# A first loop of three feature units over 1024 tokens, the sample's tile by column quarters, and the gate input copied out of its bank first

## The chip, the cores and the metric

The kernel runs on one core of a Trainium2 chip. The metric is device time in microseconds (us), the median of three runs. TensorE (PE) does the matrix products, VectorE (DVE), ScalarE (ACT) and GpSimd (POOL) the rest; SyncE (SP) issues most of the transfers. Matrix products add up in eight banks of PSUM, each of 128 partitions by 512 words of 32 bits.

## The reference, cut to what matters

One layer of a streaming encoder is run on 1024 prompt tokens and 32 sample tokens with the same weights. The part before the mixers is a modulated input and one wide projection whose columns go to three mixers (mLSTM, forgetting attention called fox here, gated MLP called gMLP):

```python
mod = silu(c) @ w_ada + b_ada                 # 6 x 1024 values for each of the two sequences
sh1, sc1, g1, sh2, sc2, g2 = split(mod, 6)
h = x * (1 + sc1) + sh1                       # x: 1024 + 32 tokens, 1024 features
mq, mk, mv, mo, mi, mf, fq, fk, fv, ff, gu, gv = split(h @ w_in, ...)
# mq, mk, mv, mo, gu, gv: 256 columns each; fq, fk, fv: 512; mi, mf: 4; ff: 8
vn = layer_norm(gv); hg = gu * (tril(ws) @ vn + bs)     # gMLP, in chunks of 128 tokens
```

The three mixers' outputs go through one output projection and a layer norm, and then through a SwiGLU feed-forward with a second layer norm. mk is scaled by 1/8 before the mLSTM uses it.

## The kernel before, in words

The tokens are one row of 1056 columns: 1024 of the prompt and the last 32 of the sample. Products are made with three passes: an operand is split into a rounded high part (fp32r) and a rest, and high x high, high x rest and rest x high are added (`gemm`, L122 to L130, and L295 to L297). `weights` (L103) loads raw weights into a ring of three buffers (`RAW`), casts the high part on ACT (L115) and subtracts for the rest on DVE or POOL (L116), each part into a ring of three (`WB`).

`fm_first` (L254) is the first loop. For each of eight k (128 features each) it makes one unit of the modulation (`ada`, L182: two halves of 512 KB of `w_ada`, sixteen TensorE instructions at L190, a copy at L193, two transposes at L196, a reduction and additions), modulates x (`h1`, L222: the load of x, L228, the casts L233, the rests L234, the sample's 32 columns in plain f32 as `hs`, L235), and adds two units of 128 output features (mq) into six banks: 512 columns, then 272 and 272, where the last 272 hold the sample. `ada(k + 1)` stands ahead of `h1(k)` in the program. The sums are copied out at L276 and L278 and stored at L280.

After the loop come units of two kinds. A `fm_unit` has 128 output features for all tokens in four parts (256, 256, 272, 272); mk is two of these, `k0` and `k1p` in `ORDER` (the p says that POOL subtracts). A `tm_unit` (L282) has token tiles of 128 as rows and 256 or 264 output columns; tiles 0 to 7 are prompt, tile 8 is the sample, made by `sample_tile` (L300) in plain f32: k modulo 4 goes to one of four strips of 32 partitions of a bank, and ACT and DVE then add the four strips (L308 to L311). Units of this kind are v of fox (twice, from `w_in_v`), v and o of the mLSTM, and the gate's two halves, G0 and G2 (`evac_gv`, L357) and G1 and G3 (`evac_gmlp`, L719).

`ORDER` is the sequence in which units (q, k, v, o, G), fox heads (f), mLSTM steps (m), further modulation units (a) and small stages (g, S, s) are emitted; f and m have higher priority, and the others fill between them. A list scheduler with a modelled timeline makes each engine's order from that. The order on an engine, SP's queue of transfers included, is then fixed.

Of the kernel before, what the change touches and what calls it, by code (L numbers as in the profile page):

```python
# [15 lines left out]
P = 128  # L16
D = 1024
KT = 8
S = 1024
T = 1056  # L20
NS = 32
# [15 lines left out]
XB, AB = (3, 6)  # L37
# [1 line left out]
MLB = (1, 2, 3, 4, 5)  # L39
RESE = "pp"  # L40
TAFF = ("aaaaaaaa", "aaaaaaav")
ORDER = "q0 f0 g q1 a f1 a g S q2 f2 k0 k1p s a q3 f3 a v q4 f4 a q5 f5 o a m0 G0 q6 f6 a m1 G1p G2p q7 m2 f7 a m3 G3"
FP = (0, 0)
RAW = 3
WB = 3
# [22 lines left out]
class Kernel:  # L68
# [184 lines left out]

    def fm_first(self, src):  # L254

        self.phase = "fm"
# [3 lines left out]
        w = None  # L260
        self.ada(0, self.p0, "araw", AB, self.pt, "t")
        for k in range(KT):
            if k < KT - 1:
                self.ada(k + 1, self.p0, "araw", AB, self.pt, "t")
            self.h1(k)
            self.phase = "fm"
            if w is None:
                w = self.weights(src, KT, 256)
            for (m, o, n), ps in zip(parts, banks):
                h, l = self.h1parts(o, n)  # L270
                self.gemm(ps[:, :n], w[k:k + 1], slice(m * P, (m + 1) * P), lambda _: h(k), lambda _: l(k),
                          start=k == 0, stop=k == KT - 1)
        out = [self.t(self.p0, [P, T], F32, "h", 2) for _ in range(2)]
        for (m, o, n), ps in zip(parts, banks):
            if m:
                self.nc.vector.tensor_copy(out[m][:, o:o + n], ps[:, :n])  # L276
            else:
                self.nc.scalar.copy(out[m][:, o:o + n], ps[:, :n])  # L278
        for m in range(2):
# [20 lines left out]
    def sample_tile(self, w, ncol, evac):  # L300

        nc = self.nc
        ps = self.t(self.pg, [P, 512], F32, "g")
        for k in range(KT):
            q = slice(k % 4 * 32, k % 4 * 32 + 32)
            nc.tensor.matmul(ps[q, :ncol], self.hs[:, k, :], w[k], start=k < 4, stop=k >= 4)
# [4 lines left out]
        nc.vector.tensor_tensor(r[:32], ps[:32, :ncol], r[:32], ALU.add)  # L311
# [45 lines left out]
    def evac_gv(self, tt, ps, n):  # L357
        nc = self.nc
        st = self.t(self.sm, [P, 6], F32, "bst", 2)
        mv = self.t(self.sm, [P, 2], F32, "bmv", 2)  # L360
        nc.vector.bn_stats(st[:n], ps[:n, :256])
        nc.vector.bn_aggr(mv[:n], st[:n])
        r = self.t(self.sm, [P, 1], F32, "brs", 2)
        self.rstd(r[:n], mv[:n, 1:2], self.eps5[:n], self.sm, "brt")
        v = self.t(self.sm, [P, 256], F32, "traw", 2)
        nc.vector.tensor_scalar(v[:n], ps[:n, :256], mv[:n, 0:1], r[:n], ALU.subtract, ALU.mult)  # L366
# [40 lines left out]
    def head_unit(self, h):  # L407

        nc = self.nc
        w = self.weights(self.d["w_in_f"][2 + h], KT, P)  # L410
# [12 lines left out]
        nc.scalar.copy(k1[lo], ps[hi])  # L423
        nc.scalar.activation(q2[lo], ps[lo], AF.Copy, scale=0.125)
        for o in (0, 256):
            kr = self.t(self.sq, [P, 272], F32, "qkr", 2)
            nc.scalar.copy(kr[hi, :256], ps[hi, o:o + 256])
            self.store(self.d["o_kT"][h, :, o:o + 256], kr[hi, :256])
        self.store(self.dqh[h, hi, :512], f(k1[hi]))
        self.lastq = self.store(self.dql[h, hi, :512], f(k2[lo]))  # L430
        if h < QD:
            evac = self.evac_qk(h)
            self.phase = "fm"
            for o, n in self.ranges((1,)):
                ps = self.t(self.pg, [P, 512], F32, "g")
                self.gemm(ps[:, :n], w, slice(0, P), *self.h1parts(o, n))
                evac(o, n, ps[:, :n])
# [280 lines left out]

    def evac_gmlp(self, tt, ps, n, bank=None):  # L719
        nc = self.nc  # L720
        if tt == 8 or tt % 2 == 0:
            self.gu = self.t(self.sm, [P, 2, 256], F32R, "vhl", 2).bitcast(F32)
            self.gbank = bank or ps
        u, z = self.gu, self.gbank
        nt = 1 if tt == 8 else 2
        nc.scalar.copy(u[:n, tt % 2], ps[:n, :256])
        if tt % 2 == 0 and tt < 8:
            return
        t0 = tt - nt + 1
# [3 lines left out]
        for g in range(4):  # L733
            q = slice(64 * g, 64 * g + 64)
            nc.tensor.matmul(z[:, :, q], self.wsp[:n, g, :n], vn[:n, :nt, q], start=True, stop=True)
# [11 lines left out]
        o = t0 * P - GO[c]  # L747
# [638 lines left out]
    def run(self):  # L1386
# [45 lines left out]
        self.fm_first(w2[0])  # L1432
        s0.close()
        after = ExitStack()
        after.enter_context(tc.issue_after(self.lastx.ins))
# [27 lines left out]
        def emit(x):  # L1463
            eng = nc.gpsimd if x[-1] == "p" else nc.vector
            x = x.rstrip("p")
            i = int(x[1:] or 0)
            if x[0] == "g":
                next(gates, None)
                return ()
            if x[0] == "f":  # L1470
                return self.fox(i, ((0, 1, 2, 3),))
            if x[0] == "m":
                return self.mlstm(i)
            if x[0] == "q":
                self.head_unit(i)
            elif x[0] == "k":
                self.fm_unit(w3[i], self.evac_mqk(2 + i, 0.125), eng=eng)
            elif x[0] == "S":
                self.sample_decay()
            elif x[0] == "G":  # L1480
                self.tm_unit(w2[3 + i % 2], 256, (self.evac_gv, self.evac_gmlp)[i % 2],
                             range(4 * (i // 2), 4 + i // 2 * 5), eng=eng)
            elif x[0] == "s":
                self.mlstm_states()
            elif x[0] == "a":
                more(1)
            else:
                self.tm_unit(w2["-vo".index(x)], 256, self.evac_raw((None, self.dmv, self.dmo)["-vo".index(x)]), eng=eng)
            return ()

        for x in ORDER.split():
# [13 lines left out]
        with tc.issue_after(self.lastq.ins):  # L1505
            self.wo_mix(0, self.KORDER[0][:6])
        for h in range(QD, PRE):
            self.fm_unit(w3[2 + h], self.evac_qk(h), (1,))
        self.wo_mix(0, self.KORDER[0][6:])
        self.z[0] = self.t(self.pz, [P, KT, GN[0]], F32, "z0", 1)  # L1510
        self.pn = self.pool("pn")
# [7 lines left out]
            weave(self.wo_range(st, *MM[0][1], (2, 6, 7, 3, 4, 5, 0, 1), kept, pw), self.ln1(0, st, *MM[0][0]))  # L1519
        weave(self.ln1(0, st, *MM[0][1]))  # L1520
        for h in range(PRE, 8):
            self.fm_unit(w3[2 + h], self.evac_qk(h, True), (1,))
        self.ln1_res(0)
        s1.close()
        s4 = ExitStack()
# [116 lines left out]
def _layout(inputs):  # L1642
# [35 lines left out]
    a["w_in"] = units(np.concatenate([mq, mv, mo, gv, gu], axis=1), 256)  # L1678
    a["w_in_f"] = units(np.concatenate([mk, qk], axis=1), 128)
# [56 lines left out]
```

## Time and profile before

| | us |
|---|---|
| median of 3 runs (lowest, highest) | 1361.67 (1360.25, 1362.21) |
| the profiled execution, its time | 1363.44 |
| its span | 1360.6 |
| TensorE busy in the span | 1328.2 (98%) |
| DVE, ACT, POOL busy | 994.9, 659.6, 233.2 |
| mean granted TensorE clock | 0.995 |

The span is the time from the first to the last instruction of the profiled execution. A TensorE row has a duration that holds the way through the array, so rows overlap, and the pace is read from the starts. One plain f32 product counts as two TensorE instructions. In the name `tm_g`, tm is the stage that allocated the tile and g its tag: g, t, s and o are PSUM banks.

### The profile page before, as it was taken

What the parts mean: (1) busy time and instruction counts of PE and PEld (TensorE: products, weight loads), DVE (VectorE), ACT (ScalarE), POOL (GpSimd) and SP (SyncE); (2) the same over time, 40 slices, a digit from 0 to 9 for tenths busy, and PEclk for the clock granted to TensorE, in tenths of its full rate; (3) what the DMA queues carried; (4) which work ended last, traced back from release to release, by engine and by line L of the source; (5) the groups of instructions that cost most, each with busy time, mean ns of one, the idle gap of its engine ahead of it and who ended that gap; (6) DMA issues with size and microseconds to landing.
All of it is one profiled execution on the core that took longest, in us unless ns stands there. A gap on an engine that the chain in (4) does not pass through costs nothing.

```text
span 1360.6 us, 25153 instructions
## 1 busy us (share of the span) xinstructions
PE 1328.2 (98%) x9434; PEld 1207.9 (89%) x9434; DVE 994.9 (73%) x2103; ACT 659.6 (48%) x1304; POOL 233.2 (17%) x263
## 2 busy tenths in 40 slices
PE   7999999998999999999999999999999999999996
PEld 4798988998989778888888888999999999999995
DVE  5545654678768668686776766778998988889777
ACT  3324454455436554545445355436663554545355
POOL 0202100053226300000000000273710000000341
PEclk9999999999989999999999999999999999999999
DMA  9775565546464866354433423674596758563321
GB/s 360 250 252 162 163 197 146 177 127 200 149 206 135 208 190 181 105 156 126 135 107 114 117 90 100 204 179 128 161 259 166 205 153 220 142 176 126 98 80 66
DMA packets 120376, 221.70 MB, mean 163 GB/s; under 512 B 18740, under 2 KB 64464, under 8 KB 120256
## 3 DMA queue, kind: packets, MB, share of 16 engines
q1 hardware_dynamic: 113024, 207.55, 48.6%
q0 software_dynamic: 6032, 11.94, 5.2%
q8 instruction: 74, 1.21, 0.4%
q10 hardware_dynamic: 1200, 0.62, 0.2%
q14 instruction: 46, 0.38, 0.1%
HBM read 188.13 MB, written 51.85 MB: 176 GB/s over the span
## 4 chain that ended last, share of the span: by engine, by line
PE 87%; DVE 5%; DMA 4%; ACT 2%; issue 1%; SPq 1%; DVEq 0%; ACTq 0%
PE up_g L130 6%; PE up_g L128 6%; PE up_g L129 6%; PE dn_g L128 4%; PE dn_g L130 4%; PE dn_g L129 4%; PE tm_g L295 3%; PE tm_g L297 3%; PE tm_g L296 3%; PE sup_u L130 3%; PE sup_u L128 3%; PE sup_u L129 3%; PE wo_g L129 2%; PE fox_t L830 2%; PE wo_g L130 2%; PE wo_g L128 2%
## 5 line engine op out<-in xcount | busy, mean ns | idle before, releaser
L128 PE MATMUL up_g<-tm_ah,up_whi 128*128 128x512 f32 (+1 forms) x384 | 140.3, 365 | 1.2 <-DVE up_sil L1186 0.8
L129 PE MATMUL up_g<-tm_al,up_whi 128*128 128x512 f32 (+1 forms) x384 | 140.8, 367 | 0.0
L130 PE MATMUL up_g<-tm_ah,up_wlo 128*128 128x512 f32 (+1 forms) x384 | 139.8, 364 | 0.5 <-DVE up_wlo L116 0.5
L1255 ACT CAST sup_whi<-sup_raw 128x1024 fp32r<-128x1024 f32 x54 | 56.0, 1048 | 90.8 <-PE dn_u L129 47.4
L115 ACT CAST up_whi<-up_raw 128x1024 fp32r<-128x1024 f32 x50 | 52.5, 1049 | 68.3 <-PE up_g L129 26.1
L128 PEld LDWEIGHTS up_g<-tm_ah,up_whi 128*128 128x128 f32 x384 | 72.2, 188 | 13.7 <-DVE up_sil L1186 1.0
L130 PEld LDWEIGHTS up_g<-tm_ah,up_wlo 128*128 128x128 f32 x384 | 72.3, 188 | 11.7 <-DVE up_wlo L116 1.2
L129 PEld LDWEIGHTS up_g<-tm_al,up_whi 128*128 128x128 f32 x384 | 72.2, 188 | 10.6
L116 DVE TENSOR_TENSOR up_wlo<-up_raw,up_whi 128x1024 fp32r<-128x1024 f32 x50 | 66.6, 1333 | 13.3 <-ACT up_whi L115 12.2
L1086 DVE SCALAR_TENSOR_TENSOR wo_z<-dn_g,start_mod,wo_z 128x512 f32<-128x512 f32 (+4 forms) x120 | 60.3, 520 | 22.0 <-PE dn_g L130 21.3
L1256 DVE TENSOR_TENSOR sup_wlo<-sup_raw,sup_whi 128x1024 fp32r<-128x1024 f32 x54 | 68.2, 1266 | 10.8 <-ACT sup_whi L1255 10.8
L130 PE MATMUL dn_g<-up_acth,dn_wlo 128*128 128x512 f32 (+2 forms) x200 | 73.7, 369 | 0.0
L129 PE MATMUL dn_g<-up_actl,dn_whi 128*128 128x512 f32 (+2 forms) x200 | 73.4, 368 | 0.0
L128 PE MATMUL dn_g<-up_acth,dn_whi 128*128 128x512 f32 (+2 forms) x200 | 73.4, 368 | 0.0
L803 ACT ACTIVATE fox_p<-fox_s,fox_fmx 128x384 f32<-128x384 f32 (+2 forms) x96 | 55.1, 578 | 37.5 <-DVE fox_fmx L801 29.4
L115 ACT CAST dn_whi<-dn_raw 128x1024 fp32r<-128x1024 f32 (+1 forms) x44 | 42.7, 971 | 55.6 <-PE up_g L129 14.4
L798 DVE TENSOR_REDUCE fox_fmx<-fox_s 128x1 f32<-128x384 f32 (+2 forms) x96 | 52.6, 552 | 20.3 <-PE fox_s L795 19.3
L835 ACT CAST fox_pth<-fox_t 128x512 fp32r<-128x512 f32 (+1 forms) x80 | 41.6, 543 | 51.1 <-PE fox_t L830 49.0
L116 DVE TENSOR_TENSOR dn_wlo<-dn_raw,dn_whi 128x1024 fp32r<-128x1024 f32 (+1 forms) x44 | 49.5, 1126 | 12.9 <-ACT dn_whi L115 12.2
L836 DVE TENSOR_TENSOR fox_ptl<-fox_t,fox_pth 128x512 fp32r<-128x512 f32 (+1 forms) x80 | 49.8, 631 | 10.0 <-ACT fox_pth L835 9.7
L295 PE MATMUL tm_g<-tm_whi,start_h1h 128*128 128x256 f32 (+1 forms) x192 | 55.1, 287 | 1.9 <-DVE tm_traw L366 1.7
L296 PE MATMUL tm_g<-tm_wlo,start_h1h 128*128 128x256 f32 (+1 forms) x192 | 55.2, 288 | 0.0
(666 smaller groups left out, 4796.5 us busy)
## 6 DMA issues: line engine op xcount, KB each, us to landing
up_raw<-w_gu SPq DMA_DIRECT2D x50, 512.0 KB
dn_raw<-w_dn SPq DMA_DIRECT2D x28, 512.0 KB
ada_late<-w_ada SPq DMA_DIRECT2D x24, 512.0 KB
sup_raw<-w_gu SPq DMA_DIRECT2D x20, 512.0 KB
start_dp<-w_gu SPq DMA_DIRECT2D x19, 512.0 KB
start_dp<-w_gu POOLq DMA_DIRECT2D x19, 512.0 KB, 7.8
wo_raw<-w_o SPq DMA_DIRECT2D x18, 512.0 KB
sup_raw<-start_dp SPq DMA_DIRECT2D x18, 512.0 KB
```

Source lines behind the costliest of these rows:

```text
L115: nc.scalar.copy(hi[:, :w], raw[:, :w])
L116: (eng or nc.vector).tensor_tensor(lo[:, :w], raw[:, :w], f(hi[:, :w]), ALU.subtract)
L128: nc.tensor.matmul(ps, hi, xh(k), start=start and k == 0, stop=False)
L129: nc.tensor.matmul(ps, hi, xl(k), start=False, stop=False)
L130: self.lastmm = nc.tensor.matmul(ps, lo, xh(k), start=False, stop=stop and k == n - 1)
L295: nc.tensor.matmul(ps[:, :ncol], xh, hi, start=k == 0, stop=False)
L296: nc.tensor.matmul(ps[:, :ncol], xh, lo, start=False, stop=False)
L798: nc.vector.tensor_reduce(mxs[:, x:x + 1], s[:, :w], AX.X, ALU.max, negate=True)
L803: nc.scalar.activation(pr[:, lo:hi], banks[x][:, :hi - lo], AF.Exp, bias=mxs[:, 0:1], accum_out=sums[:, x:x + 1])
L1086: self.lastz = self.nc.vector.scalar_tensor_tensor(z[:, m, x:y], ps[:, x - a:y - a], g[i], z[:, m, x:y], ALU.mult, ALU.add)
L1255: nc.scalar.copy(h, x)
L1256: tt(l, x, f(h), ALU.subtract)
```

## The change

The first loop takes three units (mq and the first half of mk) over the 1024 prompt tokens alone, as six parts of 512 columns. Its weights come in four chunks of two k each, 768 columns wide, and `h1(k)` and the chunk's load stand ahead of `ada(k + 1)`. The sample's 32 tokens are made from `hs` and the raw weights: after each fourth k, one matmul for each of the four k writes a strip of 32 partitions, and ACT copies the strips out. After the loop a matrix `fold` (128 x 32, a one where the partition modulo 32 is the column) adds the strips, and its result is copied behind the 1024 tokens. k0 is taken out of `ORDER`.

In the `tm_unit`s each of the sample tile's four strips has a quarter of the unit's columns for all eight k, so that nothing has to be added; four ACT copies put the quarters side by side. The second copy of the gate's sample tile goes. `evac_gv` copies its input out of the bank with ACT first, and the statistics and normalization read the copy.

```diff
-ORDER = "q0 f0 g q1 a f1 a g S q2 f2 k0 k1p s a q3 f3 a v ...
+ORDER = "q0 f0 g q1 a f1 a g S q2 f2 k1p s a q3 f3 a v ...
     def fm_first(self, src):
-        parts = [(m, o, n) for o, n in ((0, 512), (512, 272), (784, 272)) for m in range(2)]
+        N = 384
+        parts = [(m, o) for o in (0, 512) for m in range(3)]
...
+        fold = self.t(self.p0, [P, NS], F32, "fold", 1)
+        nc.vector.tensor_reduce(fold, self.ident.rearrange("p (q t) -> p t q", q=4), AX.X, ALU.add)
         self.ada(0, self.p0, "araw", AB, self.pt, "t")
+        halves = []
         for k in range(KT):
+            self.h1(k)
+            if k % 2 == 0:
+                w = self.weights(src[:, k * N:(k + 2) * N], 2, N)
+                raws = self.raws if k % 4 == 0 else raws + self.raws
             if k < KT - 1:
                 self.ada(k + 1, self.p0, "araw", AB, self.pt, "t")
-            self.h1(k)
-            if w is None:
-                w = self.weights(src, KT, 256)
...
+            if k % 4 == 3:
+                ps = self.t(self.pt, [P, 512], F32, "t")
+                for q in range(4):
+                    nc.tensor.matmul(ps[32 * q:32 * q + 32, :N], self.hs[:, k - 3 + q, :], raws[q],
+                                     start=True, stop=True)
+                halves.append(self.t(self.p0, [P, N], F32, "smq", 2))
+                nc.scalar.copy(halves[-1], ps[:, :N])
...
+        for m in range(3):
+            for i in range(2):
+                nc.tensor.matmul(ps[:, NS * m:NS * m + NS], halves[i][:, m * P:(m + 1) * P], fold,
+                                 start=i == 0, stop=i == 1)
+        for m in range(3):
+            evac[m](out[m][:, S:], ps[:, NS * m:NS * m + NS])
             self.store(self.dmqk[:, m], out[m])
...
     def sample_tile(self, w, ncol, evac):
+        n = ncol // 4
         for k in range(KT):
-            q = slice(k % 4 * 32, k % 4 * 32 + 32)
-            nc.tensor.matmul(ps[q, :ncol], self.hs[:, k, :], w[k], start=k < 4, stop=k >= 4)
-        r = self.t(self.sm, [2 * NS, 264], F32, "tmsum", 1)[:, :ncol]
-        nc.scalar.copy(r, ps[64:128, :ncol])
-        nc.vector.tensor_tensor(r, ps[:64, :ncol], r, ALU.add)
-        nc.scalar.copy(ps[:32, :ncol], r[32:64])
-        nc.vector.tensor_tensor(r[:32], ps[:32, :ncol], r[:32], ALU.add)
-        evac(8, r[:32], NS, *([ps] if evac == self.evac_gmlp else []))
+            for q in range(4):
+                nc.tensor.matmul(ps[32 * q:32 * q + 32, :n], self.hs[:, k, :], w[k][:, n * q:n * q + n],
+                                 start=k == 0, stop=k == KT - 1)
+        r = self.t(self.sm, [NS, 264], F32, "tmsum", 1)[:, :ncol]
+        for q in range(4):
+            nc.scalar.copy(r[:, n * q:n * q + n], ps[32 * q:32 * q + 32, :n])
+        evac(8, r, NS, *([ps] if evac == self.evac_gmlp else []))
     def evac_gv(self, tt, ps, n):
-        nc.vector.bn_stats(st[:n], ps[:n, :256])
+        v = self.t(self.sm, [P, 256], F32, "traw", 2)
+        nc.scalar.copy(v[:n], ps[:n, :256])
+        nc.vector.bn_stats(st[:n], v[:n])
...
-        nc.vector.tensor_scalar(v[:n], ps[:n, :256], mv[:n, 0:1], r[:n], ALU.subtract, ALU.mult)
+        nc.vector.tensor_scalar(v[:n], v[:n], mv[:n, 0:1], r[:n], ALU.subtract, ALU.mult)
```

The rest of the diff follows from this: the weights are laid out as `w_in_1` (eight k of 384 columns, for the loop), `w_in` and `w_in_f` without these columns, the indices of the later units move by one, the six sums are copied out by ACT (m = 0, and m = 2 with the scale 1/8) and DVE (m = 1), and `evac_gmlp` takes the sample's tile as it comes.

More of the change, by code (lines that the diff above doesn't have):

```diff
@@ L41 @@
 TAFF = ("aaaaaaaa", "aaaaaaav")
-ORDER = "q0 f0 g q1 a f1 a g S q2 f2 k0 k1p s a q3 f3 a v q4 f4 a q5 f5 o a m0 G0 q6 f6 a m1 G1p G2p q7 m2 f7 a m3 G3"
+ORDER = "q0 f0 g q1 a f1 a g S q2 f2 k1p s a q3 f3 a v q4 f4 a q5 f5 o a m0 G0 q6 f6 a m1 G1p G2p q7 m2 f7 a m3 G3"
 FP = (0, 0)
@@ L266, in fm_first @@
             self.phase = "fm"
-            if w is None:
-                w = self.weights(src, KT, 256)
-            for (m, o, n), ps in zip(parts, banks):
-                h, l = self.h1parts(o, n)
-                self.gemm(ps[:, :n], w[k:k + 1], slice(m * P, (m + 1) * P), lambda _: h(k), lambda _: l(k),
-                          start=k == 0, stop=k == KT - 1)
[L273 to L278, printed above, removed]
@@ L279, in fm_first @@
-        for m in range(2):
+            for (m, o), ps in zip(parts, banks):
+                h, l = self.h1parts(o, 512)
+                self.gemm(ps, w[k % 2:k % 2 + 1], slice(m * P, (m + 1) * P), lambda _: h(k), lambda _: l(k),
+                          start=k == 0, stop=k == KT - 1)
+            if k % 4 == 3:
[5 more added lines that the diff above has]
+                nc.scalar.copy(halves[-1], ps[:, :N])
@@ new lines, in fm_first @@
+        out = [self.t(self.p0, [P, T], F32, x, b) for x, b in (("h", 2), ("h", 2), ("x", XB))]
+        evac = (lambda y, x: nc.scalar.copy(y, x), lambda y, x: nc.vector.tensor_copy(y, x),
+                lambda y, x: nc.scalar.activation(y, x, AF.Copy, scale=0.125))
+        for (m, o), ps in zip(parts, banks):
+            evac[m](out[m][:, o:o + 512], ps)
+        ps = self.t(self.pt, [P, 512], F32, "t")
+        for m in range(3):
+            for i in range(2):
+                nc.tensor.matmul(ps[:, NS * m:NS * m + NS], halves[i][:, m * P:(m + 1) * P], fold,
+                                 start=i == 0, stop=i == 1)
@@ L409, in head_unit @@
         nc = self.nc
-        w = self.weights(self.d["w_in_f"][2 + h], KT, P)
+        w = self.weights(self.d["w_in_f"][1 + h], KT, P)
         self.phase = "head"
@@ L720, in evac_gmlp @@
         nc = self.nc
-        if tt == 8 or tt % 2 == 0:
+        if tt < 8 and tt % 2 == 0:
             self.gu = self.t(self.sm, [P, 2, 256], F32R, "vhl", 2).bitcast(F32)
-            self.gbank = bank or ps
+            self.gbank = ps
+        if bank:
+            self.gu, self.gbank = ps.unsqueeze(1), bank
         u, z = self.gu, self.gbank
         nt = 1 if tt == 8 else 2
-        nc.scalar.copy(u[:n, tt % 2], ps[:n, :256])
+        if tt < 8:
+            nc.scalar.copy(u[:n, tt % 2], ps[:n, :256])
         if tt % 2 == 0 and tt < 8:
@@ L1431, in run @@
         nc.vector.tensor_copy(self.c32[:, :, 0:2], self.cs)
-        self.fm_first(w2[0])
+        self.fm_first(d["w_in_1"])
         s0.close()
@@ L1476, in emit @@
             elif x[0] == "k":
-                self.fm_unit(w3[i], self.evac_mqk(2 + i, 0.125), eng=eng)
+                self.fm_unit(w3[0], self.evac_mqk(3, 0.125), eng=eng)
             elif x[0] == "S":
@@ L1480, in emit @@
             elif x[0] == "G":
-                self.tm_unit(w2[3 + i % 2], 256, (self.evac_gv, self.evac_gmlp)[i % 2],
+                self.tm_unit(w2[2 + i % 2], 256, (self.evac_gv, self.evac_gmlp)[i % 2],
                              range(4 * (i // 2), 4 + i // 2 * 5), eng=eng)
@@ L1487, in emit @@
             else:
-                self.tm_unit(w2["-vo".index(x)], 256, self.evac_raw((None, self.dmv, self.dmo)["-vo".index(x)]), eng=eng)
+                self.tm_unit(w2["vo".index(x)], 256, self.evac_raw((self.dmv, self.dmo)["vo".index(x)]), eng=eng)
             return ()
@@ L1507, in run @@
         for h in range(QD, PRE):
-            self.fm_unit(w3[2 + h], self.evac_qk(h), (1,))
+            self.fm_unit(w3[1 + h], self.evac_qk(h), (1,))
         self.wo_mix(0, self.KORDER[0][6:])
@@ L1521, in run @@
         for h in range(PRE, 8):
-            self.fm_unit(w3[2 + h], self.evac_qk(h, True), (1,))
+            self.fm_unit(w3[1 + h], self.evac_qk(h, True), (1,))
         self.ln1_res(0)
@@ L1677, in _layout @@
     qk = np.stack([fq.reshape(1024, 8, 64), fk.reshape(1024, 8, 64)], axis=2).reshape(1024, 1024)
-    a["w_in"] = units(np.concatenate([mq, mv, mo, gv, gu], axis=1), 256)
-    a["w_in_f"] = units(np.concatenate([mk, qk], axis=1), 128)
+    a["w_in_1"] = units(np.concatenate([mq, mk[:, :128]], axis=1), 384)[0]
+    a["w_in"] = units(np.concatenate([mv, mo, gv, gu], axis=1), 256)
+    a["w_in_f"] = units(np.concatenate([mk[:, 128:], qk], axis=1), 128)
     a["w_o"] = units(g["w_o"][0], 128)
```

4 lines of the change are left out of this document (1 added, 3 removed).

## The prediction

> **What bounds the kernel now.** I read the page's busy shares, then 5 us windows of the start, the chain of waits there, and TensorE's waits.
>
> ```profile
> span 1360.6 us, 25153 instructions
> PE 1328.2 (98%) x9434; PEld 1207.9 (89%) x9434; DVE 994.9 (73%) x2103; ACT 659.6 (48%) x1304; POOL 233.2 (17%) x263
> 10.00:15.00 5.00, 2.60 (x13) 0.99 (x14) 3.62 (x11) 2.96 (x6) 0.00 (x0) 1.00 1.03 417
> 20.00:25.00 5.00, 5.00 (x42) 3.77 (x40) 1.63 (x6) 0.56 (x3) 0.00 (x0) 1.00 1.03 408
> 45.00:50.00 5.00, 5.00 (x31) 4.36 (x30) 4.65 (x9) 2.58 (x7) 4.64 (x5) 1.00 0.01 4
> 120.00:140.00 20.00, 20.00 (x142) 16.09 (x141) 9.53 (x35) 8.50 (x20) 8.48 (x13) 1.00 0.60 176
> ```
>
> A window's row gives, after the stretch and its length, the busy us (and instructions) of TensorE, its weight loads, DVE, ACT and POOL, then the granted clock, the DMA share and GB/s. TensorE is busy for 98% of the span. It is already full inside the first loop, where the DMA engines are full too (share 1.03), and it is full at 120 to 140, where k0 stands between fox units. The change therefore does not move work into an idle stretch. It pays by the matmul time it takes out and the few waits it closes.
>
> ```profile
> 3.56 7.92 DMA ada_x<-xT
> 11.57 0.82 DVE ada_h L228
> 12.41 0.62 ACT start_ah L233
> 13.03 0.55 ACT start_h1h L233
> 13.70 0.95 ACT fm_whi L115
> 14.70 0.80 PE fm_g L128
> 16.35 0.43 PE fm_g L129
> 25.77 0.37 ACT ada_adas L193
> 26.15 0.53 ACT start_ah L233
> 44.09 0.22 PE ada_t L196 x2
> 45.92 0.25 PE fm_s L128 x2
> 46.29 0.23 PE fm_g L129
> 51.21 1.04 PE tm_g L306 x16
> PE tm_g L295 <- DVE tm_traw L366: 2.0, 2, 1.7
> PE tm_g L735 <- DVE tm_tmsum L311: 1.6, 1, 1.6
> ```
>
> The chain gives the pace: 0.233 us for 512 columns and 0.125 us for 272, once TensorE is up to speed; in the first 3.8 us after 14.70 it takes twice that (0.43). The granted clock is 1.00 throughout that stretch. The last two rows (TensorE's waits: total, times, longest) are the gate units' banks.
>
> **Start of the loop, -2.4 us.** The first product waits until 14.70 for the first x, its operands and the weights' cast.
>
> ```profile
> 1.66 1.85 SPq L85 DMA_DIRECT2D ada_araw<-w_ada  x4
> 5.79 2.25 PE L190 MATMUL ada_t<-ada_araw,start_c 128*32 128x256 f32 x16 [5.79 <-DMA ada_araw<-w_ada]
> 8.89 1.08 PE L190 MATMUL ada_t<-ada_araw,start_c 128*32 128x256 f32 x8 [0.85 <-DMA ada_araw<-w_ada]
> 9.90 0.69 PE L196 MATMUL ada_t<-start_ident,ada_adas 128*128 128x128 f32 x2
> 10.52 1.08 PE L190 MATMUL ada_t<-ada_araw,start_c 128*32 128x256 f32 x8
> 8.11 0.37 ACT L193 COPY ada_adas<-ada_t 128x256 f32<-128x256 f32 x1 [5.00 <-PE ada_t L190]
> ```
>
> Four halves of w_ada lie ahead of x. With h1(0) ahead of ada(1), two of them go behind it, and each takes about 1.6 us (8.89 to 10.52), so x lands near 8.4 instead of 11.57. The first modulation is then last. Its copy ends at 8.48, the transposes (0.69) no longer stand behind the second unit's matmuls, and reduction and addition (0.6 us, my allowance) take it to 9.8. With 0.82, 0.62, 0.55 and a cast of 768 instead of 1024 columns (0.95 x 0.75 = 0.7) the product starts at 12.5. That is 2.2 us sooner, or 3.4 if the cast goes ahead of x's. I take -2.4, with 0 as the other end, if the issue order stays.
>
> **Bubbles in the loop, -2.6 us.** From 14.70 to 51.2 are 36.5 us. The products are 8 x (6 x 0.233 + 12 x 0.125) = 23.2 us, the slow start adds 1.8 (half of 3.7), thirteen halves of w_ada at 0.55 (half of the 1.04 of the same shape in L306) are 7.2, and seven pairs of transposes at 0.22 are 1.5: 33.7 in all. The other 2.8 are bubbles such as the one at 25.77 to 26.72. Afterwards a step k needs 18 x 0.233 = 4.2 us plus 1.3 for its ada unit, while its 1.79 MB (two halves, x, a quarter of the weights) take 4.4 us at 408 GB/s, so TensorE is always behind the loads and the bubbles close. One wait is added: the copy of the sample's sums waits on ACT for the end of step 3, and casts of later x queued behind it would hold TensorE, by 1.0 us at most (copy 0.4, cast 0.62) if they come after it; TensorE's lag covers that if they come before. Ends: -2.8 and 0.
>
> **Columns, +1.3 us.** k0 was 96 products at 0.125 = 12.0 us. The loop's products go from 23.2 to 8 x 18 x 0.233 = 33.5. Together 35.2 become 33.5, -1.7. The sample's share comes back in plain f32: per four k, 8 instructions of 384 columns, 1.5 times the half above, so 0.8, twice is 1.5. The fold is 12 instructions with 128x128 weights and 32 columns.
>
> ```profile
> 529.91 1.09 PEld L652 LDWEIGHTS mlstm_s<-mlstm_mv,mlstm_mw 128*128 128x128 f32 x8
> 523.11 0.43 PE L922 MATMUL foxs_o<-foxs_v,foxs_pth 128*32 128x64 f32 x16
> 523.47 0.31 PE L922 MATMUL foxs_o<-start_vs,foxs_pth 32*32 32x64 f32 x8
> L306 PE MATMUL tm_g<-tm_raw,start_hs x96: 379/385/413, 51.1 to 326.9; 128*32 128x256 f32 x64, 128*32 128x264 f32 x32
> ```
>
> Eight such loads take 1.09 us, so 12 take 1.5 (0.3 at the spacing of L922, the other end). Where k0 stood, TensorE is full (the window at 120), so its 12 us leave whole, with two weight loads and four stores on SP, two casts on ACT and two subtractions on DVE. The new evictions (four copies on ACT, two on DVE, as long as the old) and third output store are nobody's wait: the stores are read only by the mLSTM steps far later.
>
> **Sample tile by quarters, six times, +2.9 us.** The 16 instructions of a tile (96 in L306) become 64 of 64 or 66 columns. L922 has the very shape: 16 start within 0.36 us (523.11 to 523.47), 22.5 ns each, four column strips in turn. 64 x 22.5 = 1.44 us against 0.96 (16 at 60 ns), +0.48 each. By columns alone it would be 0; at the 60 ns of the old ones +2.9 each, 17 in all, an end far from the matching shape. The Trainium skill ("TensorEngine Tiling (Array Packing)", Instruction Overhead) warns not to take the tiling factor from a dimension that is already small, which speaks against this edit; "TensorE: Matmul & The Clock Gate" (Wait — 56ns, not 53.3ns?) puts a floor of about 25 ns between starts, which would make the term an estimated +3.8. The trace sits slightly below that floor.
>
> **Gate units, -2.0 us.** The bank now goes free after one ACT copy, and the sample's chain loses two DVE additions. Both waits above (3.6 us) end that way, but the next thing is near:
>
> ```profile
> 333.20 0.57 ACT L423 CAST head_k<-head_g 64x512 fp32r<-64x512 f32 x1
> 334.19 0.50 PE L794 MATMUL fox_s<-head_k,head_qp 128*128 128x128 f32 x2
> L366 DVE TENSOR_SCALAR tm_traw<-tm_g,tm_bmv,tm_brs x8: 527/544/546, 271.9 to 328.3; 128x256 f32<-128x256 f32 x8
> L366 DVE TENSOR_SCALAR tm_traw<-tm_tmsum,tm_bmv,tm_brs x1: 401/401/401, 308.1 to 308.1; 32x256 f32<-32x256 f32 x1
> L325 ACT COPY tm_traw<-tm_g x16: 372/373/374, 57.2 to 105.1; 128x256 f32<-128x256 f32 x16
> ```
>
> The last head's scores at 334.19 need k, cast at 333.20 to 333.77, so a TensorE that arrives 3.6 us sooner waits there for part of it. I take -2.0, ends -3.6 and 0. The copies (nine at 0.37, 3.4 us) lie on ACT, 48% busy. They are paid back partly by L366, 0.54 us from the bank and 0.40 from SBUF. The Trainium skill ("VectorE: DVE Perf Modes", Why PSUM operands drop a tier) says the same of fp32 tensor_scalar; the trace agrees in direction.
>
> **Weights of the next unit, +0.7 us.** The raw ring has three buffers. The loop used two; now it uses four, and those of k = 4 to 7 are held to the sample matmuls at the loop's very end.
>
> ```profile
> 34.47 1.93 SPq L85 DMA_DIRECT2D tm_raw<-w_in_v  x3
> 58.00 6.50 DMA ada_late<-w_ada
> L115 ACT CAST tm_whi<-tm_raw x19: 1033/1048/1096, 47.5 to 322.1; 128x1024 fp32r<-128x1024 f32 x15, 128x1056 fp32r<-128x1056 f32 x4
> L116 DVE TENSOR_TENSOR tm_wlo<-tm_raw,tm_whi x15: 1203/1225/1651, 48.6 to 324.7; 128x1024 fp32r<-128x1024 f32 x11, 128x1056 fp32r<-128x1056 f32 x4
> ```
>
> Three loads that were issued at 34.5, under the loop, shrink to one; the second chunk of w_in_v starts only at the end of the loop. With some 3 us to land (about 1.3 for 0.54 MB at 408 GB/s, the rest my allowance) and 1.05 for its cast, TensorE waits some 4 us, less the fold (1.5) and 12 products each of three tiles' first halves (36 x 0.125 = 4.5), if the scheduler puts these first. Covered, it costs 0; uncovered, up to 6 (below).
>
> **Sum.** -2.4 - 2.6 + 1.3 + 2.9 - 2.0 + 0.7 = -2.1 us. The profiled execution took 1363.44 us (span 1360.6), 1.8 above the median 1361.67; it would become 1361.3, and the median 1359.6. A measurement tells about 0.2%, 2.7 us, from no change, so this lies just inside.
>
> **Rivals.** (1) Everything small falls well: the quarters cost their columns alone, both gate waits go whole, the next weights are covered. -2.4 - 2.6 + 1.3 + 0 - 3.6 + 0 = -7.3, 1354.4 us. For it: the full strips and the plain rows of the waits; against: L922's 22.5 ns. (2) Slower: the second weight chunk queues at the loop's end behind three output stores (1.6 MB) on SP and lands like ada_late at 58.00, after 6.5 us. With the cast that is 7.6, of which only the fold covers 1.5, so +6.1 in place of +0.7: +3.3, 1365.0 us. It decides where TensorE's order has the sample tile, which needs both chunks, first, as it had at 51.21. Against it: the scheduler moved work round waits elsewhere in the loop. (3) k0's work was cover: the fox units wait on DVE and ACT once it is gone, and half of its 12 us comes back as waiting, +3.9, 1365.6 us. Against: DVE is busy 9.5 of 20 us there. (4) The quarters run at 60 ns: +14.4 more, 1374.0 us; L922 speaks against it.
>
> **How the numbers follow.** Forecast 0.50, of which 0.20 beyond 2.7 us faster, 0.24 within, 0.06 slower (its terms' nearer ends give -5 to +1). Rival 1: 0.26; rival 2: 0.14; rival 3: 0.07; rival 4: 0.03. Faster 0.20 + 0.26 = 0.46, same 0.24, slower 0.06 + 0.14 + 0.07 + 0.03 = 0.30. The range goes from just below rival 1 to just above rivals 2 and 3: 1353.5 to 1366. The forecast's own is 1356.5 to 1362.5.
>
> **What would show it.** First product near 12.5; the first tm tile's sample matmuls near 60 (51.2 + 33.5 - 23.2 + 3.0 - 5.0 = 59.5); no ACT or DVE pieces of the chain inside the loop after k = 2. Each sample tile 1.4 to 1.6 us. No row of TensorE waiting for L366 or for the sample's additions, but perhaps one for the head's casts. TensorE's wait for a tm_raw load, or a cast behind it, right after the loop under 1 us. The forecast fails if that wait is several us, if the quarters space at 60 ns, or if TensorE shows new idle time between 110 and 140.

## The result: slower by 0.28%

The changed kernel takes 1364.53 us (median; 1362.94 to 1368.0) against 1361.63 us (1355.12 to 1364.25) for the kernel before on the same chip. The ratio is 1.0028, 95% interval 1.0015 to 1.0040: by the ratio 3.8 us slower (the two medians lie 2.9 apart), where the forecast was 2.1 us faster. The profiled execution took 1364.42 us.

Page of after: span and busy us (share, count) of each engine.

```profile
span 1362.6 us, 25618 instructions
PE 1330.8 (98%) x9654; PEld 1206.4 (89%) x9654; DVE 995.5 (73%) x2093; ACT 661.9 (49%) x1326; POOL 232.2 (17%) x263
```

Split the span into busy and idle TensorE, one execution each. Before, 1328.2 us busy leave 32.4 idle; after, 1330.8 leave 31.8. The prediction's terms for work (columns +1.3, sample tile +2.9) add up to +4.2 busy, its terms for waits (-2.4, -2.6, -2.0, +0.7) to -6.3 idle. Busy rose by 2.6, more than half of what was said. Idle fell by 0.6 only: **the work came, the waits did not go.**

Timeline of TensorE in after: start, us, instruction, count. The last instructions of w_ada ahead of the first product, this product, the sample's strips (L280) in the loop, the fold, the first sample tile.

```profile
11.74 1.08 PE L190 MATMUL ada_t<-ada_araw,start_c 128*32 128x256 f32 x8 [2.10 <-DMA ada_araw<-w_ada]
12.75 1.65 PE L128 MATMUL start_g<-start_ah,ada_whi 128*128 128x512 f32 x3
33.05 0.52 PE L280 MATMUL fm_t<-ada_raw,start_hs 128*32 128x384 f32 x2
33.39 0.49 PE L280 MATMUL fm_t<-ada_raw,start_hs 128*32 128x384 f32 x2
38.62 0.84 PE L280 MATMUL fm_t<-fm_raw,start_hs 128*32 128x384 f32 x4
51.20 0.84 PE L280 MATMUL fm_t<-fm_raw,start_hs 128*32 128x384 f32 x4
55.18 0.83 PE L280 MATMUL fm_t<-fm_raw,start_hs 128*32 128x384 f32 x2
60.55 0.83 PE L280 MATMUL fm_t<-fm_raw,start_hs 128*32 128x384 f32 x2
64.20 1.20 PE L292 MATMUL fm_t<-start_fold,fm_smq 128*128 128x32 f32 x10
65.32 1.13 PE L323 MATMUL tm_g<-tm_raw,start_hs 128*32 128x66 f32 x64
```

The first product comes at 12.75, as predicted (12.5). The first sample tile comes at 65.32, not at 59.5: the loop takes 52.6 us instead of 47.0. Adding up, for each line, the time from an instruction's start to the next one's gives products 37.3 (the prediction's figures: 33.5 + 1.8 = 35.3), w_ada 8.4 (7.2), transposes 2.2 (1.5), strips 3.4 and fold 1.3 (3.0 together): 5.6 more. A wait counts in the row in front of it. Windows of before, then of after, up to the first product and from there to the first sample tile:

```profile
0.00:14.70 14.70, 5.57 (x37) 1.42 (x37) 5.88 (x29) 4.53 (x9) 1.88 (x12) 1.00 0.82 295
14.70:51.14 36.44, 35.71 (x253) 25.89 (x253) 23.84 (x51) 14.33 (x31) 8.26 (x14) 1.00 0.83 328
0.00:12.75 12.75, 3.84 (x27) 0.93 (x27) 5.62 (x26) 3.99 (x7) 1.93 (x12) 1.00 0.80 275
12.75:65.32 52.57, 51.58 (x294) 32.91 (x290) 27.02 (x58) 18.58 (x39) 5.79 (x14) 1.00 0.67 253
```

TensorE idles for 9.1 us ahead of the first product in before and for 8.9 in after; from there to the first sample tile for 0.7 and 1.0. The prediction wanted 5.0 us less in these two stretches, and the sum is 9.9 in both kernels.

TensorE's waits in after between 10 and 70 us (total, times, longest), then those of the whole span that belong to the gate units' stretch.

```profile
PE ada_t L190 <- DMA ada_araw<-w_ada: 2.1, 1, 2.1
PE ada_t L196 <- ACT ada_adas L193: 0.6, 1, 0.6
PE ada_t L190 <- DVE ada_adam L198: 0.3, 1, 0.3
PE fox_s L814 <- ACT head_k L440: 4.2, 1, 4.2
```

In before the first product waited 1.9 us for the weights' cast; that wait is gone, and 2.1 us for w_ada, whose halves now stand behind x, are new. Both lie ahead of the first product (the row at 11.74). The gates' two waits (3.6 us) are gone, and the last head's casts are now waited for for 4.2 us.

```profile
333.19 1.59 DVE L116 TENSOR_TENSOR fm_wlo<-fm_raw,fm_whi 128x1024 fp32r<-128x1024 f32 x1
335.15 0.68 DVE L437 SCALAR_TENSOR_TENSOR head_qp<-head_g,head_qp 64x512 fp32r<-64x512 f32 x1
335.87 0.58 ACT L438 CAST head_k<-head_g 64x512 fp32r<-64x512 f32 x1 [2.69 <-DVE head_qp L437]
337.43 0.58 ACT L440 CAST head_k<-head_g 64x512 fp32r<-64x512 f32 x1
338.06 0.80 PE L814 MATMUL fox_s<-head_k,head_qp 128*128 128x128 f32 x2 [4.20 <-ACT head_k L440]
330.00:340.00 10.00, 5.74 (x50) 4.91 (x40) 8.90 (x29) 6.29 (x18) 2.73 (x5) 0.86 0.85 248
340.00:350.00 10.00, 10.00 (x68) 9.86 (x69) 6.38 (x19) 6.78 (x20) 0.73 (x1) 0.80 0.65 204
```

Timeline and windows of after: a weight subtraction of 1.59 us on DVE, then the head's own steps, and only then the scores. The granted clock (0.86, 0.80) drops there: the records give half clock for 6.8 us from 337. Before has a stretch of the same length from 378, so in these two executions it is not time added.

### The profile page after: what moved, and what is told of

It is laid out like the page before. It is cut to its first block, busy times and chain, and to the rows that moved or that the text cites. A ratio compares the mean times of both kernels' runs of the same rounds, so it can differ in the third digit from the quotient of the medians.

```text
span 1362.6 us, 25618 instructions
## 1 busy us (share of the span) xinstructions
PE 1330.8 (98%) x9654; PEld 1206.4 (89%) x9654; DVE 995.5 (73%) x2093; ACT 661.9 (49%) x1326; POOL 232.2 (17%) x263
## 4 chain that ended last, share of the span: by engine, by line
PE 66%; DVE 5%; DMA 3%; ACT 1%; issue 1%; SPq 0%; ACTq 0%; DVEq 0%
PE up_g L128 6%; PE up_g L130 6%; PE up_g L129 6%; PE dn_g L128 4%; PE dn_g L130 4%; PE dn_g L129 4%; PE sup_u L128 3%; PE sup_u L130 3%; PE sup_u L129 3%; PE wo_g L128 2%; PE wo_g L130 2%; PE wo_g L129 2%; PE sup_g L130 2%; PE sup_g L129 2%; PE sup_g L128 2%; PE fox_t L850 2%
## 5 line engine op out<-in xcount | busy, mean ns | idle before, releaser
L128 PEld LDWEIGHTS up_g<-tm_ah,up_whi 128*128 128x128 f32 x384 | 72.2, 188 | 14.2 <-ACT up_whi L115 1.6
L313 PE MATMUL tm_g<-tm_whi,start_h1l 128*128 128x256 f32 (+1 forms) x192 | 56.2, 293 | 0.0
```

What stands on the lines that cost most here:

```text
L128: nc.tensor.matmul(ps, hi, xh(k), start=start and k == 0, stop=False)
L313: nc.tensor.matmul(ps[:, :ncol], xl, hi, start=False, stop=k == 7)
```

## The experiments

Four theories are named in the expectations. A: the loss is work on TensorE that the prediction priced too low, instructions with 32 outputs in lone pieces between those with 128. B: the loss is at the end of the fox stage, where the gates' waits turn into the wait for the last head. C: changing between 32 and 128 outputs costs nothing. D, later: the loss is the scheduler's other order. Ratios are to the kernel before in the same comparison, with 95% intervals; 0.1% is 1.4 us.

**The three parts alone, and one tie.** `loop_only` is before with the new first loop, `tile_only` with the new sample tile, `gv_only` with the gate copy. `grouped` is after, with

```diff
+                n0 = len(nc.cur_bb.bb.instructions)
                 for q in range(4):
                     nc.tensor.matmul(ps[32 * q:32 * q + 32, :N], self.hs[:, k - 3 + q, :], raws[q],
                                      start=True, stop=True)
+                self.tie(nc.cur_bb.bb.instructions[n0:], self.lastmm, (mybir.EngineType.PE,))
```

so that the strips stay behind the last product of their k.

> The kernel before with the new first loop alone (three units over 1024 tokens, the sample's strips and fold, k0 out of the order); the sample tiles and the gate's evictions are the old ones. Theory A (the loss is made in the loop: the sample's f32 matmuls stand one or two at a time between products and fill one or two of four strips, and every change between a 32-column and a 128-column instruction costs some 0.2 us): 1.0 to 2.5 us over the kernel before. Rival B (the loss is made at the end of the fox stage, where the waits on the gate's banks turn into a 4.2 us wait on the last head's casts): within 0.7 us of the kernel before.

> The kernel before with only the sample tiles of the later units by quarters. Theory A: within 0.7 us of the kernel before, since an undisturbed tile takes 1.05 us against 1.00 before, and what it saves on DVE is not on the path. Rival B: it carries part of the loss, +1 to +3 us, with a wait of the last head's scores on its casts.

> The kernel before with only the gate input copied from its bank by ACT first. Theory A: within 0.7 us, the wait of TensorE on the normalization (2.0 us) gone and another in its place. Rival B: +1 to +3 us, ACT's copies ahead of the last head's casts delay the scores.

> The changed kernel, but the loop's four sample matmuls of a group are ordered behind the last product of their k, so that they stand together or nearly so. Theory A: the 3.4 us of these matmuls fall to 1.5 to 2.5 and two or three changes of the array's use go, so 1.5 to 3 us less than the changed kernel, that is 0 to +1.5 us against the kernel before. Rival B: as slow as the changed kernel, +2.5 to +3.5 us.

Measured: loop_only 1.0011 (0.9997 to 1.0025), tile_only 1.0014 (1.0003 to 1.0024), gv_only 1.0000 (0.9989 to 1.0011), grouped 1.0023 (1.0008 to 1.0037). The three parts add up to 1.0025, so the whole 1.0028 needs no interaction. grouped is 0.7 us below the changed kernel where A wanted 1.5 to 3, a miss. The gate copy gains nothing, and why stands in TensorE's waits of gv_only:

```profile
PE tm_g L736 <- DVE tm_tmsum L311: 3.4, 1, 3.4
```

The wait for the bank (2.0) is gone and the one for the old tile's additions grew from 1.6 to 3.4: 3.6 us under two names are 3.4 under one. In tile_only the additions are gone, and most of the wait has the third name (0.5 us for the bank are left):

```profile
PE fox_s L797 <- ACT head_k L423: 3.0, 1, 3.0
```

**The price of changing the outputs, by itself.** 64 extra f32 products of 32 columns (128 instructions) are put among the plain ones of the two v units of the kernel before; `dummy_strip` gives them 32 outputs, `dummy_full` 128.

```diff
+                if ncol == 264 and k % 2 == 0:
+                    nc.tensor.matmul(dm[0:32, :32], self.c32[:, k, :], self.ident[:, :32], start=True, stop=True)
```

> The kernel before with 64 extra f32 matmuls of 32 columns by 32 outputs (a strip, nothing reads them) behind every second k of the 16 prompt tiles of the two v units, most of them alone between products of 128 outputs. Theory A (a change of the array between 32 and 128 outputs costs by itself): each lone one costs 0.25 to 0.35 us from the product before to the product behind, beyond the 0.12 that lies between two products anyway; +14 to +22 us in all. Rival C (no such cost; the loss of the changed kernel is the strips' own streaming): 0.03 to 0.1 us each, +2 to +6 us.

> As dummy_strip, with f32 matmuls of 32 columns by 128 outputs instead, so that no instruction changes the array's use. Both theories: their own 0.21 us each (the fold's 12 instructions took 1.27 us, 0.106 each, two to a matmul), and no more; +13 to +14 us. Under theory A the strips, which load a quarter of the weights, cost as much or more than these; under rival C much less.

```profile
60.06 0.28 PE L297 MATMUL tm_g<-tm_whi,start_ah 128*128 128x264 f32 x1
60.28 0.44 PE L303 MATMUL tm_o<-start_ident,start_c 128*32 128x32 f32 x8
60.65 0.39 PE L298 MATMUL tm_g<-tm_wlo,start_ah 128*128 128x264 f32 x1
60.87 0.29 PE L299 MATMUL tm_g<-tm_whi,start_al 128*128 128x264 f32 x1
60.99 0.29 PE L297 MATMUL tm_g<-tm_whi,start_ah 128*128 128x264 f32 x1
```

Timeline of dummy_strip. Plain products start 0.12 us apart (60.87, 60.99). Into the strips it is 0.22 (60.06 to 60.28), and from the first product behind them to the next 0.22 again (60.65 to 60.87). Over the pieces that stand between plain products, 2, 4, 6 and 8 instructions with 32 outputs cost 0.376, 0.439, 0.501 and 0.562 us: 0.031 each and **0.31 us for going there and back**. With 128 outputs it is 0.221, 0.448, 0.670 and 0.890: 0.111 each and nothing fixed. The times are near this: 1376.09 and 1375.23 us, one execution each, against a median of 1359.31 for before, so 16.8 and 15.9 more, where 34 more pairs of changes (169 changes for 101) and 128 instructions make 34 x 0.31 + 128 x 0.031 = 14.5, and 128 x 0.111 = 14.2. C is out. The Trainium skill ("TensorEngine Tiling (Array Packing)", Key Properties) says that changing the tiling mode, though not just the tile, drains TensorE. These rows agree and give it a price.

**The sample tile kept whole, in the changed kernel.** `hp_tile` is after with the tile's 64 instructions under `tc.high_priority(2000)`; `hp_both` has grouped's tie too.

> The changed kernel with the 64 instructions of each sample tile at a high priority, so that they stand in one piece (17 pieces in the changed kernel's order become 6 and the loop's stay as they are). Theory A: 1 to 2.5 us less than the changed kernel, +1.3 to +2.8 us against the kernel before. Rival B (the wait at the end of the fox stage is the loss): as the changed kernel, +2.5 to +4.

> hp_tile and grouped together: the sample tiles in one piece and the loop's sample matmuls behind their k's products. Theory A: 2.5 to 4.5 us less than the changed kernel, -0.7 to +1.3 us against the kernel before. Rival B: as the changed kernel, +2.5 to +4.

Measured 1.0090 (1.0072 to 1.0109) and 1.0067 (1.0048 to 1.0086). Both miss by far. Each tile now takes 1.03 to 1.06 us in one piece, but the priority moved other work too, and TensorE waits elsewhere:

```profile
PE wo_g L128 <- ACT tm_ah L1041: 5.3, 1, 5.3
```

(TensorE's waits, hp_both; 2.4 in before.) TensorE idles for 36.4 us in hp_tile and 38.5 in hp_both, against 31.8 in after. As a test of the pieces these two are inconclusive.

**Parts of the loop.** `order_only` is before with only the exchange of the two steps:

```diff
         for k in range(KT):
-            if k < KT - 1:
-                self.ada(k + 1, self.p0, "araw", AB, self.pt, "t")
             self.h1(k)
...
+            if k < KT - 1:
+                self.ada(k + 1, self.p0, "araw", AB, self.pt, "t")
```

`order_gv` adds the gate copy, `no_sample` leaves the sample out of the changed kernel's loop (zeros stand for it in the three units), `grouped_loop` is loop_only with the tie above.

> The kernel before, with only the order of the first loop's two steps exchanged: h1(k) and the weights' call ahead of ada(k+1); two units on all columns, old sample tile, old gate units. By the prediction's term for the start alone the first product comes at 12.5 instead of 14.7 and nothing else changes: 1361.6 - 2.2 = 1359.4 us, ratio 0.998. Theory A (the losses of the changed loop are its f32 strips and the changes between 32 and 128 outputs) expects the same, with the first sample tile near 49 (51.1 - 2.2). The rival, loads set the pace: the loop moves the same bytes, w_ada's later halves are now behind x, so the modulations for k = 1 to 3 come later and the gain is gone by the first sample tile (51 again), ratio 1.000.

> order_only and the gate copy together: the two parts of the change that by the runs so far lose nothing, as a candidate that beats both kernels. If they add, 1359.4 us, ratio 0.998, with no wait for the gate's banks. If the earlier TensorE only waits longer at the end of the fox stage for the last head's casts (theory B), 1361, ratio 0.9995, with a wait of over 3 us for head_k.

> The changed kernel without the sample's share of the first loop: the eight strip instructions of 384 columns, their copies and the twelve instructions of the fold are left out, and the sample's columns of those three units are zeros. By the prediction's columns this is worth 1.5 + 1.5 = 3.0 us: 1361.5 us, ratio 1.0000 to the kernel before. Theory A: 3.4 + 1.3 us of matmuls and some 1.5 us in slower neighbours, the products after each change among them, 6.2 in all: 1358.3 us, ratio 0.9976, first sample tile near 59.5. Theory B (the loss is at the end of the fox stage, where an earlier TensorE waits longer): most of it is given back, 1363, ratio 1.001, with a wait of over 6 us there.

> loop_only (the kernel before with the new first loop alone) with each group of four strip instructions held together behind the last product of its step. Theory A: with 5 pieces turned into 2, three changes at 0.31 and the serial strips saved, 1.5 to 2 us: loop_only's 1.0011 becomes 0.9997 to 1.0000. Theory B expects what the after kernel's version of this tie gave, at most 0.7 us: 1.0006.

Measured: order_only 1.0011 (1.0000 to 1.0022), order_gv 1.0011 (1.0001 to 1.0022), no_sample 1.0025 (1.0013 to 1.0038), grouped_loop 0.9998 (0.9985 to 1.0012).

order_only starts its products at 12.12, 2.6 us earlier than before, and reaches the first sample tile at 53.33, 2.2 us later. In order_only, TensorE's waits between 10 and 70 us begin with the first two rows; the others are of its timeline:

```profile
PE fm_g L128 <- ACT start_ah L233: 4.1, 3, 2.6
PE ada_t L196 <- ACT ada_adas L193: 1.1, 2, 0.6
18.45 1.07 PE L190 MATMUL ada_t<-ada_araw,start_c 128*32 128x256 f32 x16
22.26 0.73 PE L128 MATMUL fm_g<-start_ah,ada_whi 128*128 128x512 f32 x2 [0.68 <-ACT start_ah L233]
```

(4.1 in place of before's 0.4; the longest, 2.6, still lies ahead of the first product.) From the first product to the first sample tile TensorE idles for 2.9 us, in before for 0.7: what x gains, the next modulations lose. The rival on record, loads that set the pace, had the outcome right. Its cause isn't shown: the modulation's instructions at 18.45 wait for no load, they stand behind the first step's products in TensorE's order, and x at 22.26 waits for them. order_gv gains nothing either; it waits for the old tile's additions for 3.4 us, and not for the head's casts.

no_sample is a test from the other side. It leaves out 4.7 us of strips and fold and reaches the first sample tile at 65.07 instead of 65.32. Its timeline and windows:

```profile
56.60 0.38 PE L196 MATMUL ada_t<-start_ident,ada_adas 128*128 128x128 f32 x2
59.14 0.97 PE L128 MATMUL start_g<-start_ah,fm_whi 128*128 128x512 f32 x3 [2.16 <-ACT start_ah L233]
62.40 0.63 PE L130 MATMUL start_g<-start_ah,fm_wlo 128*128 128x512 f32 x1
64.74 0.40 PE L130 MATMUL start_o<-start_h1h,fm_wlo 128*128 128x512 f32 x1
60.00:65.00 5.00, 5.00 (x16) 3.74 (x14) 1.51 (x4) 1.72 (x4) 0.00 (x0) 0.66 0.00 0
```

TensorE waits 2.16 us for the last step's modulated x, and then runs at half clock for 3.4 us (granted clock 0.66; a product lasts 0.63 instead of 0.40). A miss for all three expectations. TensorE's idle time in the loop rises from 1.0 to 2.8 us, and half clock for 3.4 us costs an estimated 1.7: together 3.5 of the 4.7 us come back.

**Order and tile once more, and a candidate.** `tile_whole` and `tile_whole100` are tile_only with the tile's instructions under `tc.high_priority(800)` and `(100)`; `loop_oldorder` is grouped_loop with `ada(k + 1)` ahead of `h1(k)` again; `grouped_gv` is grouped_loop with the gate copy.

> tile_only (the kernel before with the sample tile by quarters) with the 64 instructions of each tile at a priority 800 higher, so that each of the six tiles stands in one piece on TensorE. Changes between outputs of up to 32 and of 128 partitions on TensorE fall from 117 to 99 (101 in the kernel before). Theory A (a change pair costs 0.31 us): nine pairs less than tile_only, 2.8 us: ratio 1.0014 becomes 0.9993 to 1.0000, 1360 us, each tile 1.05 us. Theory D (the loss is not the pieces but the other order in which the scheduler leaves the fox units): 1.0014 or more, 1363 us.

> The same with a priority 100 higher: nine pieces in place of fifteen, 105 changes. Theory A: six pairs less than tile_only, 1.9 us: 1.0000, 1361 us. Theory D expects a time that does not follow the number of pieces: anywhere from 1.000 to 1.003.

> grouped_loop with ada(k+1) ahead of h1(k) again, as in the kernel before; the sample's eight instructions and the three units stay. The prediction's term for the start: first product at 14.7 in place of 12.6, 2.2 us slower than grouped_loop: 1362.5 us, ratio 1.0014. The rival, from order_only (the exchange alone gained nothing, its products waited 4.1 us for h1 later): no difference, 0.9998, with less waiting inside the loop. By theory A four pairs of changes less (99 for 107), which would make it up to 1.2 us faster than that.

> grouped_loop with the gate input copied from its bank first: everything of the change but the sample tile by quarters, as a candidate that beats both kernels. If the bank's waits (2.1 us for L384 in grouped_loop's trace) are gained: 0.9985, 1359 us. Theory B (the last head's casts set the end of the fox stage): 0.9998 to 1.0005, 1361 us, with a wait of 3 us or more there.

Measured: tile_whole 1.0036 (1.0022 to 1.0050), tile_whole100 1.0031 (1.0018 to 1.0045), loop_oldorder 0.9993 (0.9982 to 1.0005), grouped_gv 0.9997 (0.9987 to 1.0007).

loop_oldorder starts its products at 14.84, grouped_loop at 12.63; they reach the first sample tile at 62.24 and 62.08. Two microseconds at the start are gone within the loop, and the times cannot be told apart. loop_oldorder's waits between 10 and 70 us (all that the list has):

```profile
PE ada_t L190 <- DMA ada_araw<-w_ada: 1.0, 1, 1.0
PE ada_t L196 <- ACT ada_adas L193: 0.5, 1, 0.5
```

against 2.1 and 0.6 in grouped_loop. The waits for w_ada lie ahead of the first product in both. TensorE idles for 8.3 us up to there in loop_oldorder and for 8.8 in grouped_loop, so the 2.2 us are not idle time: 16 more of w_ada's instructions run in them, and 88 instead of 104 are left for the loop. From the first product to the first sample tile loop_oldorder needs 47.4 us and grouped_loop 49.4, with no idle time against 0.7, and the whole order has eight changes less (99 for 107). grouped_gv's wait of 4.0 us is again for the old tile's additions.

For the tile, the page of tile_only and that of tile_whole stand against each other:

```profile
span 1362.0 us, 25739 instructions
PE 1331.4 (98%) x9722; PEld 1212.3 (89%) x9722; DVE 993.1 (73%) x2091; ACT 659.3 (48%) x1315; POOL 234.9 (17%) x263
```

```profile
span 1364.4 us, 25726 instructions
PE 1328.0 (97%) x9722; PEld 1211.9 (89%) x9722; DVE 986.0 (72%) x2091; ACT 658.0 (48%) x1315; POOL 233.1 (17%) x263
```

With the tiles whole, TensorE's busy time falls by 3.4 us; theory A said 2.8. Its idle time rises from 30.6 to 36.4. A misses the time in both runs, and D is right on it: the scheduler, given another priority, leaves an order with more waits. New ones among TensorE's waits of tile_whole:

```profile
PE tm_g L295 <- DVE tm_traw L367: 3.4, 2, 3.0
PE wo_t L947 <- DVE wo_z L1090: 2.3, 1, 2.3
```

So in these two executions the pieces cost about what A says, and the new waits are worth more. No version was shown to beat the kernel before: loop_oldorder comes nearest, and its interval holds 1.

## Why the prediction was wrong, step by step

**Start of the loop, -2.4: the step that failed.** The first product moved nearly as worked out (12.75 for 14.70). What failed is that its move was counted as time won. In before TensorE works on the second modulation unit in that wait (the rows at 8.89 and 10.52); in after half of it stands behind the first product: 3.8 us of work are done ahead of it instead of 5.6, and 104 instructions of w_ada are left for the loop instead of 96. The idle time ahead of the first product fell from 9.1 to 8.9 us, since the wait for the cast has become one for w_ada (2.1 us). loop_oldorder and grouped_loop end level. So the term is worth about 0, where -2.4 stood.

**Bubbles, -2.6: failed.** There was little to close. Of the 2.8 us that the prediction put down to bubbles in before's loop, the window from 14.70 to 51.14 shows 0.7 as idle TensorE, and after's loop has 1.0. "TensorE is always behind the loads" held but for that; with the sample's work left out it failed at the last step (2.16 us in no_sample). The rest of the 2.8 was in the rows: start to start and with those waits, before's products take 27.3 us instead of the 25.0 of the sum, and its transposes 1.9 instead of 1.5. (Twelve halves and six pairs of transposes stand there, not thirteen and seven, and the 1.79 MB of a step hold an eighth of the weights, not a quarter.) A likely part of it is the price of changing outputs: from the first product to the first sample tile before goes from 128 outputs to 32 or back 19 times, after 29 times. At 0.31 us a pair these are an estimated 2.9 and 4.5 us. Tying the pieces moved loop_only from 1.0011 to grouped_loop's 0.9998, about the 1.5 to 2 us expected, though the two intervals overlap, so this part is not shown.

**Columns, +1.3: too low by 1.7.** Strips and fold took 4.7 us, not 3.0: the strips 3.4 instead of 1.5 (0.8 was taken for eight that run side by side, but they came two or four at a time, and by the rows at 38.62 and 55.18 two take as long as four, 0.8), the fold 1.3 instead of 1.5. Leaving them out in no_sample gained no time that could be told apart, since a wait and half clock took their place.

**Sample tile, +2.9: near, in another form.** Whole, a tile takes 1.03 to 1.06 us against 1.0 before, below the 1.4 to 1.6 forecast; tile_only measured +1.9 us (0.4 to 3.3). In its trace TensorE is busy for 3.2 us more than in before and idle for 1.8 less. Much of the work is pieces, as in tile_only's timeline:

```profile
298.52 0.52 PE L307 MATMUL tm_g<-tm_raw,start_hs 128*32 128x64 f32 x18
298.98 1.13 PE L636 MATMUL mlstm_s<-mlstm_mqb,mlstm_mqk 128*128 128x256 f32 x4
300.04 0.31 PE L307 MATMUL tm_g<-tm_raw,start_hs 128*32 128x64 f32 x6
300.28 0.44 PE L833 MATMUL fox_t<-start_ident,fox_p 128*128 128x128 f32 x2
300.65 0.52 PE L307 MATMUL tm_g<-tm_raw,start_hs 128*32 128x64 f32 x18
```

Before's 16 instructions were seldom interrupted (seven pieces in six tiles); 64 small ones leave more places for work of higher priority (fifteen pieces). Eight more pieces are an estimated 2.5 us.

**Gate units, -2.0: failed**, though the prediction named the reason. It saw that the head's casts come next and still granted over half of 3.6 us. In after the wait is 4.2 us, and gv_only measures 0. In after and in tile_only the chain from the last head's products through DVE and ACT to its scores sets the end of that stretch; in gv_only it is the old tile's additions.

**Weights of the next unit, +0.7:** no row waits for them in after; 0. With it rival 2 falls, and so do rival 4 (16 ns instead of 60) and rival 3: the first sample tile comes 14.2 us later than before, the fourth, behind k0's old place, only 1.0 later (229.07 for 228.05), so k0's 12 us left whole.

In sum the measured parts are loop +1.5, tile +1.9, gate 0, about +3.4 of the 3.8 us; the forecast had -3.0, +2.9 and -2.0. Not settled: how tile_only's 1.9 us divide between pieces and waits that changed their place, and the last 0.4, which lies within the intervals.

## What to carry to other kernels

Bring forward the first step of a chain that shares its engine and its loads with the next steps, and the gain is only real if the last step comes sooner; look at when the loop ends, not when it begins, and count the idle time ahead of it, since a wait may be filled with work that has to be done anyway. Where TensorE waits for three things that end within a few microseconds of each other, taking away the last two is worth what the third leaves, and that was nothing here. When small products use a quarter of the array, keep them together: a trip from 128 outputs to 32 and back cost 0.31 us here, but under a list scheduler look at idle time as well, since what keeps them together also reorders the rest.

## What the hardware showed that was not expected

Four column strips in turn run faster than the prediction's row said: 64 instructions of 64 columns in 1.03 us, 16 ns apart on average (two instructions are one f32 product). The Trainium skill ("TensorE: Matmul & The Clock Gate", Wait — 56ns, not 53.3ns?) puts a floor of about 25 ns between starts; across four strips it does not hold in these rows.

And half clock followed a wait of only 2.16 us in no_sample, for one stretch of 3.4 us. Its length does not follow the wait: it was 6.8 us in after, after a wait of 4.2, and also 6.8 in before (from 378), where the longest wait just ahead was 2.1. The same page of the Trainium skill (What's actually happening) has windows of 3413 ns. The lengths agree with one and two of them, but a whole idle window, as the page asks for, is not what the waits of 2.16 and 2.1 us are. The prediction read a granted clock of 1.00 for the slow rows at the start, but a product of 512 columns there lasts 0.63 us (15.29 in before), as at half clock in no_sample (62.40), so the 1.00 is doubtful for those rows.
